# The first input-projection round, two blocks of 128 features at once, becomes two rounds of one block

## The chip, the cores and the metric

The kernel runs on one NeuronCore of a Trainium2 chip. The metric is the device time of one execution in microseconds. It was 1379.97 us as the median of three runs (1379.35 to 1381.22). TensorE (PE) multiplies, VectorE (DVE) and ScalarE (ACT) do the elementwise work, GpSimd (POOL) issues some loads, and SyncE (SP) issues most of them.

## The reference, cut to what matters

One layer of a hybrid trunk is run for two streams of 128 tokens: a prompt (conditioning `c_ctx`) and a sample (conditioning `c`). The part that the change touches is its beginning:

```python
mod = jax.nn.silu(cvec) @ w_ada_l + b_ada_l            # 2048 -> 6 x 2048
sh1, sc1, g1, sh2, sc2, g2 = jnp.split(mod[..., None, :], 6, axis=-1)
h = modulate(rmsnorm(x, norm_w), shift, scale)         # h * (1 + scale) + shift, width 2048
p = h @ w_in_l                                         # 2048 -> 8192, split over the mixers
```

Behind it come a gated linear recurrence, a short convolution and a neighbourhood attention, their output projection, a second modulation and a SwiGLU channel mixer. All is float32.

## The kernel before, in words

All tensors stand with 128 partitions. A product in float32 accuracy is three TensorE products: weights and activations are each split into a rounded part `hi` and a rest `lo`, and hi*hi, hi*lo and lo*hi are summed. For each loaded weight tile `raw`, ACT writes `hi` (L253) and DVE `lo` (L254). The activations of the two streams stand in `hT`, four tiles of four blocks of 128 features; in each, slot 0 is `hi` and slot 1 is `lo`.

The modulation of the first norm is itself a product with weights: `ada_pe` (L318) multiplies one quarter of the 2048 conditioning features (four times 128) with 256 columns of shift and 256 of scale. I call one such call a quarter: eight matmuls 32 rows high and 256 columns wide, one load of 1 MB. Four quarters give shift and scale of 256 features (two blocks). ACT copies the result out (L338), `columns` (L341) turns it so that features stand on partitions, DVE adds the biases (L351 to L353), ACT applies scale and shift to the transposed normalised x (L484), and ACT and DVE split the result into `hT` (L488, L489).

The input projection has 16 chunks of 512 output columns. The first seven (`ORDER[:START]`) are worked in rounds over the features, since the modulation of the later features is not there yet. `ROUNDS` lists (first block, number of blocks): (0,2), (2,2), (4,4), (8,4), (12,4). In a round each of the seven chunks loads the rows of its weights for these blocks (256 KB per block), multiplies them for both streams (six matmuls of 512 columns for each block), and the two sums leave PSUM: in the first round ACT copies them into `part` (L880), in the later ones DVE adds them to it (L882). Between the chunks of a round `first_step` puts the quarters that the next round needs. The other nine chunks, and all behind them, follow without rounds.

Four things limit how far the work runs ahead. `raw` has four buffers, and each load, small or large, takes a whole one; SP issues the loads in order, and each waits for the release of the buffer four loads before it. `hi` and `lo` have three buffers each. PSUM has four sums (`acc`, two chunks), three `aux` tiles and one `ada`. Each engine works through its instructions in the order in which a scheduler put them at build time.

At the very start SP issues, in this order, the two conditioning vectors, the first quarter, x of the prompt, x of the sample (1 MB each) and three quarters; these four quarters take all four `raw` buffers. ACT squares x (L503), DVE makes the reciprocal root (L201 to L207) and normalises (L505), and PE transposes (L471).

Of the kernel before, what the change touches and what calls it, by code (L numbers as in the profile page):

```python
# [10 lines left out]
F32 = mybir.dt.float32  # L11
# [13 lines left out]
NEG = -1.0e30  # L25
RMS1 = -8192.0
START = 7
ROUNDS = [(0, 2), (2, 2), (4, 4), (8, 4), (12, 4)]


LATER_T = [12, 16, 13, 17, 14, 18, 15, 19]
# [61 lines left out]
def trunk(ctx: ExitStack, tc: tile.TileContext, a: dict):  # L93
# [144 lines left out]
    def split(src, apart=False):  # L238

        n = src.shape[1]  # L240
        with tc.high_priority(offset=ahead[0]):
            raw = sb([P, 4, CH], "raw", RAW_BUFS)
            nc.sync.dma_start(raw[:, 0:n], src)
            parts = []
            if apart:
                his, los = u8((P, 4, CH), F32R), u8((P, 4, CH), F32R)
            for j in range(n // 2):
                if apart:
                    hi, lo = his[:, 2 * j:2 * j + 2], los[:, 2 * j:2 * j + 2]
                else:  # L250
                    hi = sb([P, 2, CH], "hi", HL_BUFS, F32R)
                    lo = sb([P, 2, CH], "lo", HL_BUFS, F32R)
                nc.scalar.activation(hi, raw[:, 2 * j:2 * j + 2], AF.Copy)  # L253
                nc.vector.tensor_tensor(lo, raw[:, 2 * j:2 * j + 2], hi.bitcast(F32), op=ALU.subtract)  # L254
                parts.append((hi, lo))
        return parts

# [12 lines left out]
    def split_mm(src, acc, lhs, first, last, k0=0):  # L270

        parts = split(src)
        n = src.shape[1]
        for k in range(0, n, 2):
            products([(s, acc[s]) for s in range(2)], (k, k + 1), lhs, k0, parts, first and k == 0, last and k == n - 2)

    def last_mm(steps, acc, phase):

# [37 lines left out]
    def ada_pe(src, box, part, pieces, first, last):  # L316

        if first:  # L320
            uid[0] += 1
            box["acc"] = psum.tile([P, CH], F32, tag="ada", name=f"ada_{uid[0]}", bufs=1)
        with tc.high_priority(offset=ahead[0]):
            if part in box:
                raw = box[part]
            else:
                raw = sb([P, 4, CH], "raw", RAW_BUFS)
                nc.sync.dma_start(raw, src)
                raw = [raw[:, 0:2], raw[:, 2:4]]
        for k in range(4):  # L330
            for i, (cols, row) in enumerate(pieces):
                nc.tensor.matmul(box["acc"][32 * k:32 * k + 32, 0:cols.stop - cols.start],  # L332
                                 lhsT=cst[:, 4 * part + k, 2 - row:34 - row], rhs=raw[k // 2][:, k % 2, cols],
                                 start=first and i == 0, stop=last and i == len(pieces) - 1)
        if last:
            n = cols.stop - cols.start
            e = st()
            nc.scalar.activation(e[:, 0:n], box["acc"][:, 0:n], AF.Copy)  # L338
            return e

    def columns(e, n):  # L341

        ps = aux((P, n, 4))
        for f in range(n):
            nc.tensor.matmul(ps[:, f, :], lhsT=e[:, f * P:(f + 1) * P], rhs=sel4, start=True, stop=True)
        return ps[:, :, 0:2], ps[:, :, 2:4]

    def first_fm(v, e):
        sh, sc = columns(e, 2)
        blk = slice(2 * v, 2 * v + 2)  # L350
        nc.vector.tensor_tensor(sh_fm[1][:, blk, :], sh, bc_last(bsh[:, 0, blk], 2), op=ALU.add)  # L351
        nc.vector.tensor_tensor(sc_fm[1][:, blk, :], sc, bc_last(bsh[:, 1, blk], 2), op=ALU.add)
        nc.vector.scalar_tensor_tensor(sc_fm[1][:, blk, :], sc_fm[1][:, blk, :], 1.0, bc_last(nmw[:, blk], 2),  # L353
                                       op0=ALU.add, op1=ALU.mult)
# [109 lines left out]

    def norm_fm(xn, diag=None):

        ps = aux((P, 2, 2, P))
        for s in range(2):
            for j in range(2):
# [6 lines left out]
    def modulated(dst, ps, layer, v):  # L476

        h = st((P, 2, 2, P))
        for s in range(2):
            for j in range(2):  # L480
                k = 2 * v + j
# [25 lines left out]

    hT = [None] * 4

    def first_mod(v, part, box):  # L510

        e = ada_pe(a["w_ada1"][v, part], box, part, PAIR, part == 0, part == 3)
        if part == 3:
            spawn(first_done(v, e, norm_fm([x[:, 256 * v:256 * v + 256] for x in xt])))

    def first_done(v, e, ps):
        yield
        first_fm(v, e)
        if v % 2 == 0:
            hT[v // 2] = u8(dt=F32R)  # L520
        modulated(hT[v // 2], ps, 1, v)

    COL = {"hg0": 8, "hg1": 9, "ff0": 4, "ff1": 5, "fb0": 6, "fb1": 7, "q0": 0, "q1": 1, "v0": 2, "v1": 3,
           "cb": 10, "cc": 11, "cx": 12, "nq": 13, "nk": 14, "nv": 15}
# [330 lines left out]
            S["late"] = {"f": lambda: S["K", int(name[2])][:, :, 0, :], "q": lambda: S["qT", int(name[1])][:, 0:2, :],  # L855
                         "n": lambda: S["nq"][:, :, 0, :], "c": lambda: S["cc"][:, :, 0, :]}[name[0]]()

    firsts = [(v, p) for v in range(8) for p in range(4)][1:]

    def first_step(n):  # L860
        for v, p in firsts[:n]:
            first_mod(v, p, box)
# [95 lines left out]
    for q in range(4):  # L958
        for j in range(2):
            ps = norm_fm([x1[q][:, s, 256 * j:256 * j + 256] for s in range(2)], r2)  # L960
            modulated(h2[q], ps, 2, 2 * q + j)

    S["late"] = h2[3].bitcast(F32)[:, :, 1, 0, :]

# [156 lines left out]
```

## Time and profile before

| | |
|---|---|
| median of three runs | 1379.97 us (1379.35 to 1381.22) |
| the profiled execution | 1374.68 us, its span 1372.9 us |
| PE | 1338.6 us busy, 97% of the span |
| DVE, ACT, POOL | 872.9 us (64%), 627.4 us (46%), 132.6 us (10%) |
| mean granted TensorE clock | 0.995 |
| HBM read | 330.43 MB, 243 GB/s over the span |

The profiled execution is 5.3 us shorter than the median of the runs; sums made in the trace are compared with its own 1374.68 us. A busy share is a mean over stages with different limits; what matters below is which engine waits in the first 100 us and for what. The time of one matmul in a row is its latency; the rate is read from the length of a chain and its count.

### The profile page before, as it was taken

The numbers are of one execution on the slowest core, as the hardware profiler recorded it, in microseconds if no ns is written. First come the engines' busy times: TensorE is split into PE (matmuls) and PEld (weight loads), VectorE is DVE, ScalarE is ACT, GpSimd is POOL, SyncE is SP. The second block draws the span as 40 slices with busy tenths as digits, with TensorE's granted clock in tenths as the row PEclk, the third lists the DMA queues.
The fourth block names the chain that finished last, engine by engine and source line by source line (L and its number), as shares of the span: only waits on it lengthen the run. The fifth ranks groups of instructions, "written<-read, shape, count | busy, mean of one in ns | idle before, by whom it ended". The sixth has DMA issues, their size and how long they took to land. (4 is left out here: it accounts for less than half of the span.)

```text
span 1372.9 us, 19781 instructions
## 1 busy us (share of the span) xinstructions
PE 1338.6 (97%) x7936; PEld 1078.0 (79%) x7936; DVE 872.9 (64%) x1102; ACT 627.4 (46%) x839; POOL 132.6 (10%) x201
## 2 busy tenths in 40 slices
PE   5999999999999999999999999999999999999996
PEld 3667777797798897778788888888888888888885
DVE  3355558986977687477944888655555554455564
ACT  4433447655465443446444444444334444444442
POOL 0100001131222221001200222000000000000000
PEclk9999999999999999999999999999999999999998
DMA  8898976875787889865765677555555555555551
GB/s 349 304 357 305 343 296 220 306 289 200 290 303 254 312 313 357 311 262 192 268 227 187 219 271 245 214 184 189 203 201 207 190 192 197 184 184 186 204 193 62
DMA packets 54381, 335.39 MB, mean 244 GB/s; under 512 B 7249, under 2 KB 7313, under 8 KB 19217
## 3 DMA queue, kind: packets, MB, share of 16 engines
q1 hardware_dynamic: 42768, 296.79, 59.0%
q0 software_dynamic: 10944, 36.29, 7.6%
q8 instruction: 62, 1.02, 0.3%
q10 hardware_dynamic: 576, 1.05, 0.2%
q14 instruction: 31, 0.25, 0.0%
HBM read 330.43 MB, written 3.67 MB: 243 GB/s over the span
## 5 line engine op out<-in xcount | busy, mean ns | idle before, releaser
L267 PE MATMUL acc<-hi,u 128*128 128x512 f32 x2944 | 741.2, 393 | 2.0 <-ACT u L488 1.1
L254 DVE TENSOR_TENSOR lo<-raw,hi 128x1024 fp32r<-128x1024 f32 x368 | 448.6, 1223 | 346.5 <-ACT hi L253 339.2
L267 PEld LDWEIGHTS acc<-hi,u 128*128 128x128 f32 x2944 | 548.7, 188 | 138.1 <-issue 10.4
L253 ACT ACTIVATE hi<-raw 128x1024 fp32r<-128x1024 f32 x368 | 388.8, 1060 | 544.2 <-PE acc L267 426.7
L267 PE MATMUL acc<-lo,u 128*128 128x512 f32 x1472 | 397.1, 390 | 1.8 <-DVE lo L254 1.7
L267 PEld LDWEIGHTS acc<-lo,u 128*128 128x128 f32 x1472 | 275.5, 188 | 63.0 <-DVE lo L254 3.7
L415 DVE SCALAR_TENSOR_TENSOR aacc<-araw,cs,aacc 128x512 f32<-128x512 f32 x224 | 159.0, 746 | 42.9 <-DMA araw<-w_ada 38.8
L308 PE MATMUL acc<-u,hi 128*128 128x256 f32 x768 | 142.2, 286 | 0.0
L308 PEld LDWEIGHTS acc<-u,hi 128*128 128x128 f32 x768 | 119.2, 191 | 9.7 <-issue 5.0
L308 PE MATMUL acc<-u,lo 128*128 128x256 f32 x384 | 108.3, 286 | 0.0
L332 PE MATMUL ada<-raw,cst 128*32 128x256 f32 (+1 forms) x784 | 83.7, 484 | 11.3 <-DMA raw<-w_ada 11.3
L298 ACT ACTIVATE hi<-raw 128x1024 fp32r<-128x1024 f32 x48 | 50.9, 1059 | 63.7 <-PE acc L308 34.5
L308 PEld LDWEIGHTS acc<-u,lo 128*128 128x128 f32 x384 | 72.8, 191 | 5.0 <-issue 4.2
L411 POOL COPY araw<-u 128x2 f32<-128x2 f32 x56 | 51.4, 920 | 257.7 <-DVE aacc L415 195.6
L299 DVE TENSOR_TENSOR lo<-raw,hi 128x1024 fp32r<-128x1024 f32 x48 | 58.2, 1218 | 15.3 <-ACT hi L298 12.0
L332 PEld LDWEIGHTS ada<-raw,cst 128*32 128x32 f32 x784 | 23.8, 114 | 38.0 <-issue 27.7
L882 DVE TENSOR_TENSOR u<-u,acc 128x512 f32<-128x512 f32 x56 | 35.9, 682 | 25.0 <-PE acc L267 24.9
L412 POOL DMA_DIRECT2D araw<-w_ada x56 | 30.0, 536 | 15.0 <-POOL araw L411 14.4
L405 POOL COPY aacc<-u 128x2 f32<-128x2 f32 x7 | 3.2, 453 | 266.6 <-DVE u L882 163.6
L484 ACT ACTIVATE st<-aux,sh,sc 128x128 f32<-128x128 f32 x48 | 18.1, 455 | 12.8 <-DVE sc L353 10.6
L267 PE MATMUL acc<-u,u 128*128 128x512 f32 x96 | 22.1, 389 | 0.0
L267 PEld LDWEIGHTS acc<-u,u 128*128 128x128 f32 x96 | 18.0, 188 | 3.7
(218 smaller groups left out, 627.0 us busy)
## 6 DMA issues: line engine op xcount, KB each, us to landing
raw<-w_ada SPq DMA_DIRECT2D x66, 1024.0 KB, 7.1
raw<-w_gate SPq DMA_DIRECT2D x44, 1024.0 KB, 4.8
raw<-w_up SPq DMA_DIRECT2D x44, 1024.0 KB, 4.8
raw<-w_down SPq DMA_DIRECT2D x44, 1024.0 KB, 4.8
raw<-w_in SPq DMA_DIRECT2D x33, 1024.0 KB, 6.8
araw<-w_ada POOLq DMA_DIRECT2D x56, 512.0 KB, 5.9
raw<-w_infm SPq DMA_DIRECT2D x24, 1024.0 KB, 5.6
raw<-w_out SPq DMA_DIRECT2D x16, 1024.0 KB, 7.2
```

What stands on the lines that cost most here:

```text
L253: nc.scalar.activation(hi, raw[:, 2 * j:2 * j + 2], AF.Copy)
L254: nc.vector.tensor_tensor(lo, raw[:, 2 * j:2 * j + 2], hi.bitcast(F32), op=ALU.subtract)
L267: nc.tensor.matmul(acc, lhsT=lhs[:, s, x, k0 + k, :], rhs=w[:, k % 2, :], start=first and k == ks[0] and w is hi and x == 0, stop=last and ...
L298: nc.scalar.activation(hi, raw[:, 4 * j:4 * j + 4], AF.Copy)
L299: nc.vector.tensor_tensor(lo, raw[:, 4 * j:4 * j + 4], hi.bitcast(F32), op=ALU.subtract)
L308: nc.tensor.matmul(one, lhsT=w[:, k % 4, ws], rhs=y, start=first and k == 0 and i == 0, stop=last and k == 7 and i == 2)
L332: nc.tensor.matmul(box["acc"][32 * k:32 * k + 32, 0:cols.stop - cols.start], lhsT=cst[:, 4 * part + k, 2 - row:34 - row], rhs=raw[k // 2][ ...
L411: nc.gpsimd.tensor_copy(raw[:, :, 0:1], S["late"][:, :, 0:1])
L412: nc.gpsimd.dma_start(raw, a["w_ada2"][c - 8, part // 2, :, 2 * (part % 2):2 * (part % 2) + 2, :])
L415: nc.vector.scalar_tensor_tensor(acc[:, s, :], raw[:, k, :], cs[:, 2 * part + k, s:s + 1], acc[:, s, :], op0=ALU.mult, op1=ALU.add)
L484: nc.scalar.activation(h[:, s, j, :], ps[:, s, j, :], AF.Identity, bias=bias, scale=scale)
L882: nc.vector.tensor_tensor(part[name][:, s, :], part[name][:, s, :], acc[s], op=ALU.add)
```

## The change

The list of rounds begins with two rounds of one block. So that the first of them does not need the modulation of both blocks, the shift and scale of blocks 0 and 1 are now made apart: each by four half quarters (128 columns of shift and 128 of scale, a load of 512 KB) from a new array `w_ada0`, in which the columns are laid out accordingly. Loads, splits, transposes and modulation take the number of blocks as an argument. A half quarter's load writes 1 KB pieces (256 columns of each of four rows) into the 2 KB rows of a `raw` buffer. The weights of one block are a load of 256 KB.

```diff
-ROUNDS = [(0, 2), (2, 2), (4, 4), (8, 4), (12, 4)]
+ROUNDS = [(0, 1), (1, 1), (2, 2), (4, 4), (8, 4), (12, 4)]
...
-            for j in range(n // 2):
+            for j in range((n + 1) // 2):
+                m = min(n, 2)
...
-                nc.scalar.activation(hi, raw[:, 2 * j:2 * j + 2], AF.Copy)
-                nc.vector.tensor_tensor(lo, raw[:, 2 * j:2 * j + 2], hi.bitcast(F32), op=ALU.subtract)
+                nc.scalar.activation(hi, raw[:, 2 * j:2 * j + m], AF.Copy)
+                nc.vector.tensor_tensor(lo, raw[:, 2 * j:2 * j + m], hi.bitcast(F32), op=ALU.subtract)
...
-                nc.sync.dma_start(raw, src)
+                nc.sync.dma_start(raw[:, :, 0:src.shape[2]], src)
...
-    def first_fm(v, e):
-        sh, sc = columns(e, 2)
-        blk = slice(2 * v, 2 * v + 2)
+    def first_fm(k0, n, e):
+        sh, sc = columns(e, n)
+        blk = slice(k0, k0 + n)
...
-        ks = slice(2 * (v % 2), 2 * (v % 2) + 2)
+        ks = slice(k0 % 4, k0 % 4 + n)
...
-    PAIR = [(slice(0, 256), 0), (slice(256, 512), 2)]
-    ada_pe(a["w_ada1"][0, 0], box, 0, PAIR, True, False)
+    def first_ada(k0, n, part):
+
+        src = a["w_ada0"][k0, part] if n == 1 else a["w_ada1"][k0 // 2 - 1, part]
+        return ada_pe(src, box, part, [(slice(0, n * P), 0), (slice(n * P, 2 * n * P), 2)], part == 0, part == 3)
+
+    first_ada(0, 1, 0)
...
-    firsts = [(v, p) for v in range(8) for p in range(4)][1:]
+    firsts = [(k0, n, p) for k0, n in [(0, 1), (1, 1)] + [(k, 2) for k in range(2, 16, 2)] for p in range(4)][1:]
...
-    first_step(4 * ROUNDS[0][1] // 2 - 1)
+    first_step(3)
...
-        nxt = 4 * ROUNDS[ri + 1][1] // 2 if ri + 1 < len(ROUNDS) else 0
+        nxt = 4 * max(ROUNDS[ri + 1][1] // 2, 1) if ri + 1 < len(ROUNDS) else 0
```

The scheduler's order on each engine changes in the first part of the program only: on PE within the first 870 of some 6,900 matmuls, on ACT and DVE within the first 180 instructions, and from there on it is the same; on POOL it is the same from the first to the last instruction. SP has eleven loads more.

On ACT, ahead of the first product of the projection, the order before was this (`hi` is the split of a weight tile, `st` from `ada` the copy of the modulation, `st` from `aux` the modulated x, `u_22` the tile `hT`):

```order
L503 ACTIVATE u_12_131,ssq_11_130<-u_5_112 128x2048
L253 ACTIVATE hi_201<-raw_199 128x1024
L338 ACTIVATE st_176<-ada_99 128x256
L253 ACTIVATE hi_224<-raw_222 128x1024
L484 ACTIVATE st_190<-aux_178,sh_95,sc_97 128x128 x4
L488 ACTIVATE u_22_189<-st_190 128x2x256
L253 ACTIVATE hi_270<-raw_268 128x1024
```

In the changed kernel it is this:

```order
L510 ACTIVATE u_12_131,ssq_11_130<-u_5_112 128x2048
L254 ACTIVATE hi_196<-raw_194 128x512
L339 ACTIVATE st_176<-ada_99 128x128
L254 ACTIVATE hi_213<-raw_211 128x512
L486 ACTIVATE st_187<-aux_178,sh_95,sc_97 128x128 x2
L254 ACTIVATE hi_253<-raw_251 128x512
L490 ACTIVATE u_22_186<-st_187 128x2x128
```

Two modulations stand where four stood, every instruction but the square is half as long, and the split of the third chunk's weights has moved ahead of the copy into `hT`.

On PE, between the first round and the second, the order before was this (`acc` are the chunk sums, `ada` a quarter, `aux` from `sel` the columns, `aux` from `ident` transposes):

```order
L267 MATMUL acc_402<-lo_407,u_22_189 128x512
L267 MATMUL acc_403<-lo_407,u_22_189 128x512
L345 MATMUL aux_425<-sel_72,st_395 128x4 x2
L332 MATMUL ada_460<-raw_461,cst 32x256 x8
L471 MATMUL aux_547<-ident,u_4_110 128x128 x2
L471 MATMUL aux_547<-ident,u_5_112 128x128 x2
L332 MATMUL ada_460<-raw_493,cst 32x256 x8
L267 MATMUL acc_438<-hi_442,u_22_189 128x512
```

In the changed kernel, between its first and second round, it is this:

```order
L268 MATMUL acc_359<-hi_363,u_22_186 128x512 x2
L346 MATMUL aux_376<-sel_72,st_354 128x4
L473 MATMUL aux_525<-ident,u_4_110 128x128 x2
L473 MATMUL aux_525<-ident,u_5_112 128x128 x2
L268 MATMUL acc_359<-lo_364,u_22_186 128x512
L268 MATMUL acc_360<-hi_363,u_22_186 128x512 x2
L268 MATMUL acc_360<-lo_364,u_22_186 128x512
L333 MATMUL ada_418<-raw_419,cst 32x256 x8
L268 MATMUL acc_386<-hi_390,u_22_186 128x512
```

The columns and transposes now stand inside the last chunk of the round, and one quarter instead of two stands between the rounds.

## Rows read from the trace of the kernel before

**Rows 1.** The page: the span and the engines' busy time

```profile
span 1372.9 us, 19781 instructions
...
PE 1338.6 (97%) x7936; PEld 1078.0 (79%) x7936; DVE 872.9 (64%) x1102; ACT 627.4 (46%) x839; POOL 132.6 (10%) x201
```

**Rows 2.** Stages: length, busy of PE, PEld, DVE, ACT, POOL, clock, DMA

```profile
0.00:27.03 27.03, 11.37 (x93) 5.04 (x93) 10.41 (x34) 11.47 (x16) 2.88 (x10) 0.95 0.88 341
27.03:40.00 12.97, 12.97 (x61) 9.68 (x58) 4.07 (x4) 6.60 (x10) 3.85 (x10) 0.84 0.90 342
40.00:57.77 17.77, 16.68 (x116) 10.63 (x115) 5.80 (x10) 11.30 (x20) 0.00 (x0) 1.00 0.84 284
57.77:88.65 30.88, 29.45 (x195) 20.28 (x196) 16.16 (x24) 9.04 (x13) 0.00 (x0) 1.00 0.90 328
88.65:100.00 11.35, 10.58 (x70) 7.44 (x69) 6.18 (x10) 4.98 (x8) 0.00 (x0) 1.00 1.00 406
100.00:200.00 100.00, 100.00 (x610) 74.66 (x609) 57.16 (x76) 41.24 (x55) 0.00 (x0) 1.00 0.85 320
```

**Rows 3.** PE in order of time: the start and the second round's start

```profile
7.15 1.96 PE L332 MATMUL ada<-raw,cst 128*32 128x256 f32 x16 [7.15 <-DMA raw<-w_ada]
...
19.30 0.69 PE L471 MATMUL aux<-ident,u 128*128 128x128 f32 x2
19.92 1.61 PE L332 MATMUL ada<-raw,cst 128*32 128x256 f32 x16
...
22.35 0.61 PE L345 MATMUL aux<-sel,st 128*128 128x4 f32 x4 [0.82 <-ACT st L338]
...
25.14 1.96 PE L332 MATMUL ada<-raw,cst 128*32 128x256 f32 x16 [1.68 <-DMA raw<-w_ada]
27.03 4.53 PE L267 MATMUL acc<-hi,u 128*128 128x512 f32 x10
...
55.00 0.66 PE L471 MATMUL aux<-ident,u 128*128 128x128 f32 x4
...
57.77 1.21 PE L267 MATMUL acc<-hi,u 128*128 128x512 f32 x4 [1.09 <-ACT u L488]
60.41 1.09 PE L332 MATMUL ada<-raw,cst 128*32 128x256 f32 x16 [1.43 <-DMA raw<-w_ada]
...
66.19 1.09 PE L332 MATMUL ada<-raw,cst 128*32 128x256 f32 x16
```

**Rows 4.** ACT and DVE in order of time, first 65 us

```profile
9.74 1.91 ACT L503 ACTIVATE u<-u 128x2048 f32<-128x2048 f32 x1 [5.60 <-DMA u<-xp]
...
12.23 1.91 ACT L503 ACTIVATE u<-u 128x2048 f32<-128x2048 f32 x1 [0.49 <-DMA u<-xs]
...
16.79 1.29 DVE L505 TENSOR_SCALAR u<-u,r_g 128x2048 f32<-128x2048 f32 x1
...
22.06 1.22 DVE L254 TENSOR_TENSOR lo<-raw,hi 128x1024 fp32r<-128x1024 f32 x1 [3.98 <-ACT hi L253]
...
23.46 0.16 DVE L353 SCALAR_TENSOR_TENSOR sc<-sc,nmw 128x4 f32<-128x4 f32 x1
23.66 1.50 ACT L484 ACTIVATE st<-aux,sh,sc 128x128 f32<-128x128 f32 x4 [0.36 <-DVE sc L353]
25.19 0.63 ACT L488 ACTIVATE u<-st 128x512 fp32r<-128x512 f32 x1
...
32.78 1.06 ACT L880 ACTIVATE u<-acc 128x512 f32<-128x512 f32 x2
...
63.81 1.28 DVE L882 TENSOR_TENSOR u<-u,acc 128x512 f32<-128x512 f32 x2 [4.75 <-PE acc L267]
```

**Rows 5.** The chain that ended last: 768 products on end

```profile
905.95 174.10 PE acc L267 x768
```

**Rows 6.** Loads: first 130 us, then the last 8 us: count, size, landing

```profile
raw<-w_ada SPq DMA_DIRECT2D x24, 1024.0 KB, 6.4
...
raw<-w_in SPq DMA_DIRECT2D x14, 512.0 KB, 5.7
...
o_ys<-u SPq DMA_DIRECT2D x2, 256.0 KB, 3.1
```

**Rows 7.** Who waited for whom in the first 100 us

```profile
ACT hi L253 <- DMA raw<-w_in: 35.3, 13, 7.4
```

More of the change, by code (lines that the diff above doesn't have):

```diff
@@ L250, in split @@
                 else:
-                    hi = sb([P, 2, CH], "hi", HL_BUFS, F32R)
-                    lo = sb([P, 2, CH], "lo", HL_BUFS, F32R)
-                nc.scalar.activation(hi, raw[:, 2 * j:2 * j + 2], AF.Copy)
-                nc.vector.tensor_tensor(lo, raw[:, 2 * j:2 * j + 2], hi.bitcast(F32), op=ALU.subtract)
+                    hi = sb([P, 2, CH], "hi", HL_BUFS, F32R)[:, 0:m]
+                    lo = sb([P, 2, CH], "lo", HL_BUFS, F32R)[:, 0:m]
+                nc.scalar.activation(hi, raw[:, 2 * j:2 * j + m], AF.Copy)
+                nc.vector.tensor_tensor(lo, raw[:, 2 * j:2 * j + m], hi.bitcast(F32), op=ALU.subtract)
                 parts.append((hi, lo))
@@ L274, in split_mm @@
         for k in range(0, n, 2):
-            products([(s, acc[s]) for s in range(2)], (k, k + 1), lhs, k0, parts, first and k == 0, last and k == n - 2)
+            products([(s, acc[s]) for s in range(2)], range(k, min(k + 2, n)), lhs, k0, parts, first and k == 0, last and k + 2 >= n)
     def last_mm(steps, acc, phase):
@@ L465, in norm_fm @@
     def norm_fm(xn, diag=None):
-        ps = aux((P, 2, 2, P))
+        n = xn[0].shape[1] // P
+        ps = aux((P, 2, n, P))
         for s in range(2):
-            for j in range(2):
+            for j in range(n):
                 if diag is None:
@@ L474, in norm_fm, with modulated @@
         return ps
-    def modulated(dst, ps, layer, v):
-        h = st((P, 2, 2, P))
+    def modulated(dst, ps, layer, k0, n):
+        h = st((P, 2, n, P))
         for s in range(2):
-            for j in range(2):
-                k = 2 * v + j
+            for j in range(n):
+                k = k0 + j
                 scale, bias = sc_fm[layer][:, k, s:s + 1], sh_fm[layer][:, k, s:s + 1]
@@ L508, in trunk, with first_mod, first_done @@
     hT = [None] * 4
-    def first_mod(v, part, box):
-        e = ada_pe(a["w_ada1"][v, part], box, part, PAIR, part == 0, part == 3)
+    def first_mod(k0, n, part):
+        e = first_ada(k0, n, part)
         if part == 3:
-            spawn(first_done(v, e, norm_fm([x[:, 256 * v:256 * v + 256] for x in xt])))
-    def first_done(v, e, ps):
+            spawn(first_done(k0, n, e, norm_fm([x[:, P * k0:P * (k0 + n)] for x in xt])))
+    def first_done(k0, n, e, ps):
         yield
[L518 to L521, printed above, removed]
+        first_fm(k0, n, e)
+        if k0 % 4 == 0:
+            hT[k0 // 4] = u8(dt=F32R)
+        modulated(hT[k0 // 4], ps, 1, k0, n)
     COL = {"hg0": 8, "hg1": 9, "ff0": 4, "ff1": 5, "fb0": 6, "fb1": 7, "q0": 0, "q1": 1, "v0": 2, "v1": 3,
@@ L856, in consume_fm @@
                          "n": lambda: S["nq"][:, :, 0, :], "c": lambda: S["cc"][:, :, 0, :]}[name[0]]()
-    firsts = [(v, p) for v in range(8) for p in range(4)][1:]
+    firsts = [(k0, n, p) for k0, n in [(0, 1), (1, 1)] + [(k, 2) for k in range(2, 16, 2)] for p in range(4)][1:]
     def first_step(n):
-        for v, p in firsts[:n]:
-            first_mod(v, p, box)
+        for one in firsts[:n]:
+            first_mod(*one)
         del firsts[:n]
-    first_step(4 * ROUNDS[0][1] // 2 - 1)
+    first_step(3)
     pump()
@@ L960, in trunk @@
             ps = norm_fm([x1[q][:, s, 256 * j:256 * j + 256] for s in range(2)], r2)
-            modulated(h2[q], ps, 2, 2 * q + j)
+            modulated(h2[q], ps, 2, 4 * q + 2 * j, 2)
     S["late"] = h2[3].bitcast(F32)[:, :, 1, 0, :]
@@ L1092 @@
     first = w_ada[:, :2 * D].reshape(D, 2, 8, 256).transpose(0, 2, 1, 3).reshape(D, 2 * D)
+    first0 = tiles(first)[0]
     rows = np.concatenate([np.arange(1024), np.arange(1536, 2048), np.arange(1024, 1536)])
@@ L1098 @@
         "s0": x["state_hgrn"][0, 0], "cT": np.ascontiguousarray(fm(cvec).transpose(0, 2, 1)),
-        "w_ada1": tiles(first), "w_ada2": tiles(w_ada[:, 2 * D:]),
+        "w_ada0": np.stack([np.concatenate([first0[..., h * P:h * P + P], first0[..., 256 + h * P:256 + h * P + P]], axis=-1)
+                            for h in range(2)]),
+        "w_ada1": tiles(first)[1:], "w_ada2": tiles(w_ada[:, 2 * D:]),
         "b_ada": x["b_ada"], "bsh": fm(x["b_ada"][0, :2 * D].reshape(2, D)), "nmw": fm(x["norm_mix_w"][0]), "w_in": tiles(w_in),
```

## The prediction

> **What bounds the kernel now.** I read the page first: PE is busy 1338.6 of 1372.9 us [rows 1], so the time is PE's work plus 34.3 us in which PE has none. The stages say where [rows 2]: PE is idle for 15.7 us (27.03 less 11.37) before the first product of the projection at 27.03, for 1.1 us up to 57.77 (the start of the round of blocks 2 and 3), 1.4 us up to 88.65 (the start of blocks 4 to 7), 0.8 us up to 100, and not at all in the 100 us that follow. Besides, the granted clock is at its lower level (1.2 GHz) in part of the second stage, whose mean is 0.84. So PE bounds the kernel from 57.77 on, and only the start can give something back. What is won there should come out at the end as it is: behind the first sixth of each engine's instructions the order is the same as before, and a stage in which PE does not wait moves as a whole.
>
> The order of time on PE shows the start [rows 3]: a quarter at 7.15, three more as their loads land, the last at 19.92; columns at 22.35; then a fifth quarter at 25.14, which already belongs to the next blocks, and the first product. ACT and DVE show what stands between [rows 4]: x of the sample at 12.23, normalised at 18.08 (16.79 + 1.29), shift and scale ready at 23.62, four modulations until 25.16, the copy into `hT` until 25.82. That the fifth quarter fills the wait matters: a first product that is earlier by some us does not win these us, as work that now stands ahead of it has to be done later.
>
> **The change, step by step.** I walk PE forward in the new order with durations of these rows, to a point where both kernels have the same work behind them.
>
> Step 1, the first product. The two loads of x stand 2.49 us apart (12.23 less 9.74) [rows 4], so 1 MB takes 2.49 us there. The first load is half as large, so x of the sample is there at 12.23 - 1.25 = 10.98, and its normalised copy, with the same 5.85 us, at 16.83. The other three half quarters (1.5 MB) land 3.7 us behind x, at 14.7, where 19.92 stood. So the load is no longer last, x is. From 16.83: a transpose (half of 0.69) until 17.2 and columns (half of 0.61) until 17.5. DVE has two splits in front (half of 1.22 each) until 18.1, then three small ones (about 0.46) until 18.6. ACT does two modulations (half of 1.50) until 19.4, then the third chunk's split, which the new order puts in front (0.53, half of the 1.06 for two equally long copies), until 19.9, then the half copy (0.32) until 20.2; 0.3 for the hops between engines. First product: 20.5, which is 6.5 us earlier.
>
> The unknown here is a load that writes 1 KB pieces. One bound is no loss: the 256 KB outputs at the end go in small pieces too and landed in 3.1 us, half of what the larger loads in a full queue took [rows 6]. The other is half speed, as if the empty half of each row were moved too: then the four half quarters take 5.0 us more, the last is there at 19.7, and the first product comes near 23.5 (19.7, 0.7 for itself, 0.2 copy, 0.3, 0.5, 0.75, 0.5, 0.3 and hops), 3 us of the gain gone. I take no loss, since the output row is nearest in size, and keep the other for the range.
>
> Step 2, the round of block 0. A product takes 174.10 / 768 = 0.227 us [rows 5]. A quarter costs 1.25 us: from 60.41 to 66.19 are 5.78 us, and in them 20 products (4.53). A half quarter is between 0.55 (half of 1.09) and 1.25; I take 0.7 (1.25 less half of 1.09). PE has 42 products (9.5), three half quarters (2.1), one quarter (1.25), columns (0.3) and four transposes (0.66): 13.8 us. The clock: the first ten products took 4.53 us where they need 2.27 [rows 3], and the quarter ahead 1.96 instead of 1.09; the same low stretch now costs 2.3 + 0.5. That makes 16.6, and the second round starts at 37.1. Beside it, hidden: ACT with 14 copies and seven splits of 0.53 and a half modulation, 12.4 us; SP with its issues; the adds of the sums are not there yet.
>
> Step 3, the round of block 1. 42 products (9.5), three quarters inside (3.75), columns (0.5), transposes (0.66) and one quarter behind (1.25): 15.7 us. DVE is nearly as long: 14 adds of 0.64, seven splits of 0.61 and the small ones, 14.1 us. These adds are new work (9.0 us, as one more round empties its sums); cover is there, because DVE was busy for 9.9 of the 30.7 us from 27.03 to 57.77 [rows 2], but a split that stands behind four adds makes PE wait. I put 1.1 us for that and for a late quarter; its bounds are 0 and the 2.5 us (1.09 + 1.43) that PE loses at the same place before. The round of blocks 2 and 3 then starts at 53.9.
>
> Step 4, the comparison. At 53.9 PE has done 84 products and 9 quarters (8 half ones count 4). Before, at 57.77, it has done 84 and 10. One quarter more makes 55.15 against 57.77: 2.6 us. Right behind it the kernel before waits 1.43 us for the eleventh quarter's load [rows 3]; in the walk this load is there about 2 us ahead of PE, so that stall goes too: 4.0 us. What is late next is PE itself. Against its own time: 1374.68 - 4.0 = 1370.7, the span 1368.9. The runs stand 5.3 us above the profiled one, so I forecast 1379.97 - 4.0 = 1376.0. About 0.2% (2.8 us) is what a measurement of this kernel can tell from no change.
>
> **The rivals.** First, the clock stays at its upper level (2.4 GHz). Before, it was low in the ten products behind a gap of PE of 1.68 us [rows 3]; in the new start the half quarter of the next block cuts that gap into two of about 1 us. Then the low stretch does not cost its 2.3 us: 1373.7. Against it: PE also does less in each of the first 20 us. TensorE: Matmul & The Clock Gate of the Trainium skill, section What's actually happening, says that the throttled state is the default and activity releases it; no row here shows what shorter gaps do.
>
> Second, DMA takes PE's place and the gain shrinks below what can be measured. ACT waited for weights 35.3 us in the first 100 [rows 7], so loads come just in time already. Up to the last load of round 1 there are 13.5 MB (x 2, eight half quarters 4, four quarters 4, 14 loads 3.5), in my walk landed at 48.2, and by the start of blocks 4 to 7 another 12.5 MB. PE wants that at 88.65 - 4.0 - 1.1 (a split) = 83.6, which needs 0.353 MB/us. The stage up to 88.65 moved 328 GB/s and the one behind it 406 [rows 2]. At 406 the data is 4 us early; at 328 it takes 38.1 us, and blocks 4 to 7 start at 87.4: a gain of 1.3, 1378.7. For it speaks the stage's own number; against it that PE hardly waited there, so that the buffers, not the DMA, set the 328. Half-speed 1 KB pieces end near the same time.
>
> Third, slower: the ring of four `raw` buffers limits the two small rounds. A load of 256 KB takes as much of it as one of 1 MB. From 20.5 to 53.9 there are 22 loads, 1.52 us each, so a buffer may take 6.1 us from its issue to the next. If a load lands in 6.4 us as the large ones do, with its two splits (0.53 and 0.61) it takes 7.54, 1.47 too long: 22 x 1.47 / 4 = 8.1 us are lost, 4.1 slower, 1384.1. It decides from 6.8 us on (no gain; slower by 0.2% from 7.3); with the 5.7 us of the 512 KB loads [rows 6] it is just there. For it speaks that half the bytes landed only 0.7 us sooner; against it, that a small load waits behind fewer bytes, and 3.1 us were enough for 256 KB. A rule speaks for this rival: the Trainium skill's DMA: Bandwidth & Descriptors, section Measured (HBM to SBUF), asks for loads of at least 1 MiB for 75% of the peak, and its section Anatomy of one DMA gives each load about 2.0 us besides its bytes. By that, if nothing of the fixed part overlapped, the eleven added loads would cost an estimated 22 us, which would make the kernel some 18 us slower. The trace agrees only in part, since 341 GB/s over a first stage of mixed sizes [rows 2] show that fixed parts overlap while several loads are in flight.
>
> **How the numbers follow.** The forecast gets 0.46; its own range is 1374.5 to 1377.5 (waits of step 3 between its bounds, half quarter between its bounds). The clock gets 0.15, DMA 0.28, the ring 0.11. Faster by over 0.2%: 0.39 of the forecast's 0.46, all of the clock's 0.15, 0.02 of the DMA's, 0.56. Slower: 0.11. The rest, 0.33, within 0.2%. The range 1373.2 to 1380.6 leaves out the ring and the lower half of the clock's case.
>
> **What would show it.** In the changed profile the first product should stand at 20.5 (19.5 to 22), directly behind ACT's copy and not behind a load; the granted clock should return to 2.4 GHz near 25; the second round should start near 37.1, the round of blocks 2 and 3 near 53.9, that of blocks 4 to 7 near 84.6. DMA should be less than half busy around 25 to 32 and full from 50 to 80. Behind 100 us every stage should be as long as before. Wrong would be: a first product near 23.5 (1 KB pieces); PE waiting for ACT's splits in the two small rounds with DMA idle (the ring), or in blocks 2 and 3 with DMA full (the DMA); or a stage behind 100 us that is longer by some us.

## The result, and the profile after

The changed kernel takes 1391.92 us (median of four runs, 1389.4 to 1393.61); the kernel before took 1379.66 us beside it. The ratio is 1.0087, 95% interval 1.0064 to 1.0111: slower by 12.3 us, where 1376.0 was forecast. The two profiled executions stand further apart (1393.53 and 1374.68 us), because that of before lies 5 us under its median; sizes below are taken from medians where there are any.

The page, and the stages cut as in [rows 2] (length; busy time of PE, PEld, DVE, ACT, POOL; clock; DMA share; GB/s):

```profile
span 1391.8 us, 19970 instructions
...
PE 1348.9 (97%) x8000; PEld 1082.1 (78%) x8000; DVE 882.3 (63%) x1127; ACT 628.9 (45%) x848; POOL 128.4 (9%) x201
```

```profile
0.00:27.03 27.03, 11.30 (x109) 7.07 (x110) 9.67 (x35) 10.14 (x15) 2.88 (x10) 1.00 0.78 263
27.03:40.00 12.97, 11.00 (x75) 8.02 (x73) 4.81 (x11) 10.35 (x21) 3.31 (x10) 1.00 0.80 229
40.00:57.77 17.77, 15.54 (x103) 10.07 (x104) 11.06 (x18) 4.76 (x10) 0.00 (x0) 0.90 0.88 295
57.77:88.65 30.88, 28.69 (x206) 18.93 (x206) 17.90 (x28) 10.85 (x17) 0.00 (x0) 1.00 0.99 360
88.65:100.00 11.35, 9.82 (x61) 6.89 (x62) 5.55 (x9) 6.66 (x11) 0.00 (x0) 0.85 0.93 382
100.00:200.00 100.00, 100.00 (x588) 70.97 (x588) 52.45 (x67) 34.78 (x46) 0.00 (x0) 1.00 0.76 300
```

Against [rows 2], DMA moves less in the first 40 us, not more: 263 and 229 GB/s where it moved 341 and 342. Only in the third stage is it slightly more, 295 where it moved 284. PE is idle for 4.2 us from 27.03 to 57.77 instead of 1.1. And in the 100 us behind, where PE never waits in either kernel, it passes 588 instructions instead of 610. The same stretch of time need not hold the same work in both, but counted by products (below) the loss is there too: something has become longer without a wait. These are two separate losses.

PE in order of time, to hold against [rows 3]:

```profile
22.87 2.08 PE L268 MATMUL acc<-hi,u 128*128 128x512 f32 x4 [1.92 <-ACT u L490]
...
40.87 1.48 PE L333 MATMUL ada<-raw,cst 128*32 128x256 f32 x16 [2.84 <-DMA raw<-w_ada]
42.29 2.82 PE L268 MATMUL acc<-hi,u 128*128 128x512 f32 x6
...
61.64 2.18 PE L268 MATMUL acc<-hi,u 128*128 128x512 f32 x8
```

The first product is early, at 22.87. The second round starts only at 42.29, behind 2.84 us of waiting for a quarter's load, and the round of blocks 2 and 3 at 61.64, 3.9 us later than before. The chain that ended last holds the 768 products of [rows 5] with the same 174.10 us, 19.54 us later:

```profile
925.49 174.10 PE acc L268 x768
```

Who waited for whom in the first 100 us, on PE and on SP's queue (in total, times, longest), first in the kernel before, then in the changed one:

```profile
PE ada L332 <- DMA raw<-w_ada: 10.3, 3, 7.2
...
SPq L243 <- PE ada L332: 16.5, 10, 3.0
```

```profile
PE ada L333 <- DMA raw<-w_ada: 18.4, 7, 6.5
...
SPq L243 <- PE ada L333: 27.4, 14, 3.7
```

SP stands 27.4 us with a load of projection weights (L243) that may not be issued until PE has used up the quarter that holds the buffer, four loads earlier; before it was 16.5 us.

### The profile page after: what moved, and what is told of

Same layout as the page of the kernel before. It is cut to its first block, busy times and chain, and to the rows that moved or that the text cites. A ratio compares the mean times of both kernels' runs of the same rounds, so it can differ in the third digit from the quotient of the medians.

```text
span 1391.8 us, 19970 instructions
## 1 busy us (share of the span) xinstructions
PE 1348.9 (97%) x8000; PEld 1082.1 (78%) x8000; DVE 882.3 (63%) x1127; ACT 628.9 (45%) x848; POOL 128.4 (9%) x201
## 4 chain that ended last, share of the span: by engine, by line
PE 85%; DMA 7%; issue 3%; DVE 2%; POOL 1%; ACT 1%; SPq 0%; POOLq 0%; DVEq 0%; ACTq 0%
PE acc L268 69%; PE acc L309 8%; PE ada L333 5%; DMA araw<-w_ada 3%; DMA raw<-w_ada 2%; PE aux L457 1%; DMA raw<-w_in 1%; POOL araw L412 1%; DMA aacc<-b_ada 1%; PE aux L637 0%; DVE aacc L416 0%; PE aux L380 0%; DVE lo L255 0%; PE aux L346 0%; PE aux L691 0%
## 5 line engine op out<-in xcount | busy, mean ns | idle before, releaser
L255 DVE TENSOR_TENSOR lo<-raw,hi 128x1024 fp32r<-128x1024 f32 (+1 forms) x375 | 449.5, 1203 | 326.3 <-ACT hi L254 312.7
L254 ACT ACTIVATE hi<-raw 128x1024 fp32r<-128x1024 f32 (+1 forms) x375 | 389.9, 1044 | 557.4 <-PE acc L268 428.6
L333 PE MATMUL ada<-raw,cst 128*32 128x256 f32 (+2 forms) x848 | 88.1, 457 | 20.2 <-DMA raw<-w_ada 20.1
L299 ACT ACTIVATE hi<-raw 128x1024 fp32r<-128x1024 f32 x48 | 50.6, 1059 | 63.6 <-PE acc L309 37.2
L889 DVE TENSOR_TENSOR u<-u,acc 128x512 f32<-128x512 f32 x70 | 45.1, 683 | 46.3 <-PE acc L268 46.3
L300 DVE TENSOR_TENSOR lo<-raw,hi 128x1024 fp32r<-128x1024 f32 x48 | 58.4, 1222 | 14.8 <-ACT hi L299 11.8
L333 PEld LDWEIGHTS ada<-raw,cst 128*32 128x32 f32 x848 | 27.3, 114 | 50.6 <-issue 25.2
```

Source lines behind the costliest of these rows:

```text
L254: nc.scalar.activation(hi, raw[:, 2 * j:2 * j + m], AF.Copy)
L255: nc.vector.tensor_tensor(lo, raw[:, 2 * j:2 * j + m], hi.bitcast(F32), op=ALU.subtract)
L299: nc.scalar.activation(hi, raw[:, 4 * j:4 * j + 4], AF.Copy)
L300: nc.vector.tensor_tensor(lo, raw[:, 4 * j:4 * j + 4], hi.bitcast(F32), op=ALU.subtract)
L889: nc.vector.tensor_tensor(part[name][:, s, :], part[name][:, s, :], acc[s], op=ALU.add)
```

## Experiments

All were timed beside the kernel before, which took 1378.8 to 1381.1 us in these sets. A ratio below is to the kernel before of the same set; medians of different sets are less comparable. In the first four expectations "pieces" are the 1 KB pieces that a half quarter's load writes; in the later ones they are the groups into which PE's order cuts a quarter.

**Each half of the change alone.** Rounds whole, modulation of blocks 0 and 1 in half quarters:

```diff
-ROUNDS = [(0, 1), (1, 1), (2, 2), (4, 4), (8, 4), (12, 4)]
+ROUNDS = [(0, 2), (2, 2), (4, 4), (8, 4), (12, 4)]
-    first_step(3)
+    first_step(7)
```

> The first round takes both blocks again, as in the kernel before; only the modulations of blocks 0 and 1 stay apart (eight half quarters in 1 KB pieces instead of four quarters). Ring theory (the four raw buffers count loads, so the two rounds of small weight loads leave the DMA idle and PE waits): nearly all of the loss of 12.3 us is gone, 1379 to 1383 us. Piece theory (the half quarters and their 1 KB pieces cost the time): most of the loss stays, 1388 to 1392. Extra-round theory (one more round with its boundary and its adds costs PE directly): 1379 to 1382.

Measured: 1388.53 us, ratio 1.0057 (1.0041 to 1.0073). Rounds of one block with whole quarters:

```diff
-        src = a["w_ada0"][k0, part] if n == 1 else a["w_ada1"][k0 // 2 - 1, part]
+        src = a["w_ada1"][k0 // 2, part]
-    first_ada(0, 1, 0)
+    first_ada(0, 2, 0)
-        nxt = 4 * max(ROUNDS[ri + 1][1] // 2, 1) if ri + 1 < len(ROUNDS) else 0
+        nxt = (2, 2, 8, 8, 8, 0)[ri]
```

> The two rounds of one block stay, but blocks 0 and 1 are modulated together by four whole quarters as in the kernel before, two later quarters in each of the two rounds. Ring theory: the first product comes near 26 to 27 us, the loads of 256 KB still hold a raw buffer each, 1386 to 1392 us. Piece theory: 1379 to 1382. Extra-round theory: 1385 to 1392, with PE waiting at the boundary between the two rounds and not inside them; under the ring theory it waits for loads inside them and in the round of blocks 2 and 3.

Measured: 1389.45 us, 1.0077 (1.0056 to 1.0098), inside the numbers of the ring and of the extra round. Each half costs most of the whole, so neither is the cause by itself; what they share comes first into question. The ring's number for the first was missed: its eight half quarters take whole buffers too, and its order has the same new groups on PE (below).

**The 1 KB pieces.** The half quarter lands in one run of 4 KB per partition:

```diff
-                nc.sync.dma_start(raw[:, :, 0:src.shape[2]], src)
+                raw = raw.rearrange("p k n -> p (k n)")[:, 0:4 * src.shape[2]].rearrange("p (k n) -> p k n", k=4)
+                nc.sync.dma_start(raw, src)
```

> The changed kernel, but a half quarter's load writes the buffer in one piece of 4 KB per partition instead of four of 1 KB. Piece theory: the first product comes 2 to 3 us earlier (near 20.5) and most of the loss goes, 1380 to 1386 us. Ring theory: at most 1 to 2 us, 1389 to 1392, with the idle stretches of the DMA between 20 and 37 us as before. Extra-round theory: 1391 to 1392.

Measured: 1391.25 us, 1.0078 (1.0060 to 1.0095). The first product comes 0.9 us earlier than in the changed kernel (21.98), not 2 to 3, and in this kernel the pieces cost no time that can be told at the end. They do cost DMA rate while DMA is the limit, which it is from 10 to 15 us (before, then the changed kernel):

```profile
10.00:15.00 5.00, 0.00 (x0) 0.00 (x0) 2.91 (x11) 3.75 (x4) 0.00 (x0) 1.00 1.01 421
```

```profile
10.00:15.00 5.00, 1.63 (x21) 0.98 (x25) 3.44 (x14) 3.11 (x4) 0.00 (x0) 1.00 1.08 361
```

At a share of 1.08 the 1 KB pieces move 361 GB/s, where whole quarters move 421 at 1.01 and the runs of 4 KB in this experiment move 373 at 0.94.

**The ring.** The one-block loads take buffers of two other tags, with two buffers each, so that the four `raw` buffers hold the quarters:

```diff
+            if n == 1:
+                small[0] += 1
+                raw = sb([P, 2, CH], ("ld", "araw")[small[0] % 2], 2)
+            else:
                 raw = sb([P, 4, CH], "raw", RAW_BUFS)
```

> The changed kernel, but the weight loads of the two rounds of one block go to four other buffers that have no work yet (those of the later input loads), so that the raw buffers hold modulation loads alone there. Ring theory: the DMA stays busy from 20 to 40 us, the first product comes near 21 us, the round of blocks 4 to 7 near 88, and most of the loss is gone: 1377 to 1383 us. Piece theory and extra-round theory: as the changed kernel, 1389 to 1393.

Measured: 1382.1 us, 1.0014 (1.0000 to 1.0027): 9.8 us of the 12.3 are back. The extra round and its adds are all still there, so they are not what cost the time. The DMA page of 20 to 40 us (share in tenths and GB/s in 40 slices, then the sum), of the changed kernel and of this one:

```profile
DMA  3689997436988256421038999999899479679989
...
DMA packets 2863, 4.61 MB, mean 230 GB/s; under 512 B 273, under 2 KB 1826, under 8 KB 2735
```

```profile
DMA  9999999999999899899998999989999999999999
...
DMA packets 3222, 7.53 MB, mean 377 GB/s; under 512 B 323, under 2 KB 1811, under 8 KB 2732
```

The same loads wait for a buffer in the first kernel, where DMA falls under a tenth near 29.5 us, and fill the DMA in the second. The 2.9 MB that are missing after 40 us take 7.7 us at 377 GB/s. With the loads in time, PE comes near the prediction's walk: the first product stands at 20.86 (20.5 in the walk), the second round at 38.7 (37.1), the round of blocks 2 and 3 at 53.5 (53.9) and that of blocks 4 to 7 at 86.6 (84.65), where before had 88.65 and the changed kernel 96.80.

The clock column shows the lower level (1.2 GHz) nowhere in the first 100 us of this run, and in the changed kernel from 41.4 to 44.9 and from 92.6 to 96.1, behind gaps of PE of 2.84 and 1.00 us. At full speed these two stretches would take about half (an estimate: 3.4 us less); this is a part of what the ring costs there. But the first products are slow in this run too, 0.46 us each for the first six:

```profile
20.86 2.93 PE L273 MATMUL acc<-hi,u 128*128 128x512 f32 x6 [0.84 <-ACT u L495]
23.59 0.74 PE L273 MATMUL acc<-lo,u 128*128 128x512 f32 x2
```

**The quarters on PE.** 2 us over before are left with the spare tags, and the place is seen by counting products (line of the products, busy time and count from 0 to a moment; before, then the changed kernel, then this one):

```profile
0.00:88.00 88.00, 44.03 (x168) 32.00 (x168) 0.96 0.88 326
0.00:236.50 236.50, 166.68 (x672) 124.48 (x672) 0.99 0.84 315
```

```profile
0.00:97.00 97.00, 47.86 (x169) 33.65 (x170) 0.96 0.89 308
0.00:252.00 252.00, 172.07 (x672) 125.33 (x672) 0.99 0.80 295
```

```profile
0.00:86.50 86.50, 44.79 (x168) 31.16 (x168) 1.00 0.93 338
0.00:241.50 241.50, 169.09 (x672) 123.13 (x672) 1.00 0.82 308
```

From product 168 to 672 before takes 148.5 us, both others 155, and so do the two halves of the change (155.5 and 155). PE's order of the quarters there differs: the same 141 matmuls stand in 19 groups between products before, in 24 in all of these, and they hold PE for 27.9 us instead of 22.3. PE in order of time, before and after:

```profile
103.12 1.09 PE L332 MATMUL ada<-raw,cst 128*32 128x256 f32 x16
104.14 1.21 PE L267 MATMUL acc<-hi,u 128*128 128x512 f32 x4
```

```profile
108.15 1.05 PE L333 MATMUL ada<-raw,cst 128*32 128x256 f32 x6
109.14 1.21 PE L268 MATMUL acc<-lo,u 128*128 128x512 f32 x4
110.28 1.07 PE L333 MATMUL ada<-raw,cst 128*32 128x256 f32 x10
111.28 2.11 PE L268 MATMUL acc<-hi,u 128*128 128x512 f32 x8
...
116.03 0.62 PE L333 MATMUL ada<-raw,cst 128*32 128x256 f32 x2
116.58 1.20 PE L268 MATMUL acc<-lo,u 128*128 128x512 f32 x4
...
153.80 1.06 PE L333 MATMUL ada<-raw,cst 128*32 128x256 f32 x8
154.79 0.73 PE L268 MATMUL acc<-hi,u 128*128 128x512 f32 x2
```

(A matmul of a quarter leaves two records, so x16 is the quarter's eight.) From its start to the next start a whole quarter takes 1.02 us; cut into 6 and 10 records it takes 0.99 and 1.00, and one half of it, 8 records, 0.99. A single matmul takes 0.55. To see whether the cuts make the 155, the quarters' matmuls were given a higher priority, with which the scheduler cuts fewer (21 groups), in three kernels:

```diff
-        for k in range(4):
-            for i, (cols, row) in enumerate(pieces):
+        with tc.high_priority(offset=400):
+            for k in range(4):
+                for i, (cols, row) in enumerate(pieces):
```

On the changed kernel, its ring as it was:

> Edit: the changed kernel, ring of four raw buffers kept, with only the higher priority for the quarters' matmuls: from the 168th to the 504th product 16 groups instead of 19; the first 168 products keep 6, 4 and 7 groups as in the changed kernel.
> Piece theory: 3 to 4 us less than the changed kernel, 1387 to 1389; from product 168 to 672 about 151 to 152 us; the waits for w_ada before product 168 (about 18 us) stay.
> Rival, ring theory alone (all of the loss is the wait for loads before product 168): no gain, 1391 to 1392.

Measured: 1386.61 us, 1.0047 (1.0031 to 1.0063); 148.0 us from product 168 to 672, with 22.8 us of PE for the quarters. On the kernel with the spare tags:

> Edit: the kernel with the two spare tags for single-block loads, and the 141 matmuls of the quarters issued at a higher priority, so that PE's order cuts fewer quarters in two: from the 168th to the 504th product the quarters stand in 16 groups instead of 19 (before the change 14), behind it in 5 as before.
> Piece theory (a quarter that the order cuts into more groups costs about 1 to 1.3 us per extra group): from product 168 to product 672 it takes about 151 to 152 us instead of 155, and the time falls from 1382.1 to 1378 to 1380.
> Rival, extra-load theory (the 6.5 us between these products do not come from the cuts, but from what the deeper load pattern leaves behind): still 155 us there, time 1381 to 1383.

Measured: 1377.56 us, 0.9990 (0.9971 to 1.0009); 147.5 us. Both stages are shorter than the 151 to 152 us expected, and no longer than before's although 21 groups stand where 19 stood: the 21 are 16 whole quarters and 5 whole groups of a later modulation on the same line (four matmuls of 512 columns each). So it is the cuts that cost, not the number of groups. The two cures add up about: 9.8 for the ring, 5.3 for the cuts, 14.4 for both. On the kernel before:

> Edit: the kernel before, same loads, same buffers, quarters' matmuls at the higher priority: on the whole of PE's order the quarters stand in 66 groups instead of 72.
> Piece theory (0.95 us of TensorE time per group, from 121 groups and 130.3 us against 72 groups and 83.7 us): TensorE time of the quarters 77 to 79 us, time 1373 to 1376.
> Ring theory alone: groups do not matter, 1379 to 1381.

Measured: 1378.55 us, 0.9990 (0.9968 to 1.0012). The piece theory's time was missed: the quarters' TensorE time fell from 83.7 to 76.4 us, but the time hardly. PE asks for the quarters earlier there and waits 17.7 us for their loads over the run, instead of 11.3, and for DVE in two later places (3.8 and 3.3). And with offset 30, which cuts more:

> Edit: the kernel before, same loads and same buffers, only the quarters' matmuls at a slightly higher priority, which here cuts them into more groups: behind product 168 4, 4, 13 and 7 instead of 4, 3, 7 and 5 (28 against 19); before product 168 21 against 18.
> Piece theory (1 to 1.3 us per group): from product 168 to 672 157 to 160 us instead of 148.5, time 1389 to 1394.
> Rival (a cut costs next to nothing, what differs is elsewhere): 148 to 150 us there, time 1379 to 1382.

Measured: 1433.08 us, 1.0380 (1.0358 to 1.0401), far over both numbers. In this stage it lost only 5 us (153.5), as many of its pieces are single matmuls, which are cheap; the rest comes from the later part of the program, which the edit cuts too. All quarters of the run, before and here (busy us, mean ns):

```profile
L332 PE MATMUL ada<-raw,cst 128*32 128x256 f32 (+1 forms) x784 | 83.7, 484 | 11.3 <-DMA raw<-w_ada 11.3
```

```profile
L333 PE MATMUL ada<-raw,cst 128*32 128x256 f32 (+1 forms) x784 | 130.3, 486 | 16.1 <-DMA raw<-w_ada 16.1
```

The same 784 records in 121 groups instead of 72 hold PE 46.6 us longer, 0.95 us per group, and the run is 53 us longer.

**Why a cut costs that much.** Either each change between the two kinds of matmul has a fixed price, or the four matmuls of different column groups (the 32 output partitions `32 * k`) run beside each other, and a piece is as long as a column group that has both of its matmuls in it. The loops are exchanged, so that a piece of four has one of each:

```diff
-        for k in range(4):
-            for i, (cols, row) in enumerate(pieces):
+        for i, (cols, row) in enumerate(pieces):
+            for k in range(4):
```

> Edit: the changed kernel with the two loops of a quarter's matmuls exchanged: first the four column groups' matmuls for shift, then the four for scale, where each column group had its shift and its scale on end. The same matmuls, loads and buffers; the order of the rest moves slightly (22 groups of quarters behind product 168 instead of 24).
> Column theory (the four 32-column groups of a quarter run beside each other, each with two matmuls on end, so a piece of 2 to 8 matmuls lasts 1.0 us and one matmul 0.55): a piece of up to four matmuls of different column groups now lasts 0.5 to 0.65 us, a whole quarter still 1.0 to 1.1; from product 168 to 672 150 to 152 us instead of 155, time 1386 to 1389.
> Rival, fixed price (each change between 128-row products and 32-row matmuls costs about 1 us by itself): pieces of 2 to 4 matmuls last 1.0 us as before, 153 us for two groups fewer, time 1389 to 1391.

Measured: 1385.23 us, 1.0034 (1.0013 to 1.0055), and 148.5 us from product 168 to 672. PE in order of time:

```profile
104.34 0.64 PE L333 MATMUL ada<-raw,cst 128*32 128x256 f32 x8
104.91 1.20 PE L268 MATMUL acc<-lo,u 128*128 128x512 f32 x4
...
127.57 1.07 PE L333 MATMUL ada<-raw,cst 128*32 128x256 f32 x16
128.57 1.21 PE L268 MATMUL acc<-lo,u 128*128 128x512 f32 x4
```

Half a quarter, the same 8 records, now takes 0.57 us instead of 0.99, and a whole one 1.00, so two halves cost 0.14 over the whole, where 6 and 10 records cost 0.97. A fixed price near 1 us is out; the gain is slightly above what the column theory expected. The Trainium skill says the same in TensorEngine Tiling (Array Packing), Key Properties: different tiles of the array can work in parallel. By that, four matmuls on four column groups last as long as one, and the trace agrees: 0.57 for four, 0.55 for one.

**What the early start is worth.** The same tags for the two-block loads, once on the kernel before (`if n == 2`) and once on the changed one (`if n <= 2`), without and with the priority:

> Edit: the kernel before, with only the loads of the two-block rounds sent to the two other tags (so that the ring of four holds quarters alone there). PE's groups of quarters behind product 168 are those of before (4, 3, 7, 5); between product 84 and 168 there are 7 instead of 9.
> Ring theory: PE's waits for w_ada before product 168 fall from about 4 us to under 1 (the first wait at 8 us stays), product 168 starts at 84 to 86 instead of 88; piece theory: two groups fewer are worth 2 more, and from 168 to 672 it takes 148 to 149 us as before. Together 1375 to 1378 against 1380.
> Rival (the loads were paced by the memory and not by buffers): within 1 us of before, 1379 to 1381.

> Edit: the changed kernel with the loads of both one-block rounds and of the two-block round on the two other tags, priorities as they were: 72 groups of quarters against 70 of the kernel before with the same tags.
> If the one-block start is worth its earlier products once ring and groups are out of the way: 1372 to 1376 against 1374.8 (3 us earlier at product 168, 2 us back for two groups).
> Rival (the extra half quarters, 64 more matmul records of 0.13 to 0.17 us beside their groups, and the interleaving eat it): 1376 to 1380.

> Edit: the kernel before with the two-block rounds' loads on the two other tags and the higher priority for the quarters' matmuls: 65 groups against 70 with the tags alone.
> Piece theory: about 5 us under the tags alone (1374.8), 1369 to 1371.
> Rival (waits for loads come back where the quarters are asked for earlier): 1373 to 1376.

> Edit: as the one before, with the higher priority for the quarters' matmuls: 66 groups against 65 of the kernel before with both edits.
> If the one-block start is worth its earlier products: 1367 to 1370, 1 to 3 us under the kernel before with both edits.
> Rival (it is worth nothing): level with it or up to 3 us over it, 1370 to 1373.

Measured: before with the tags 1374.78, ratio 0.9964 (0.9950 to 0.9978); changed 1376.34, 0.9978 (0.9962 to 0.9994). With the priority too: 1376.51, 0.9976 (0.9961 to 0.9992), missed by 5 us as above, and 1376.01, 0.9973 (0.9953 to 0.9994), missed as well. No gain for the early start shows in either pair. The tags alone make the kernel before faster by 5.5 us too, so its ring also held loads back, and not all of the 9.8 us above is a cost of the change. The tags and the exchanged loops together, first on the kernel before:

> Edit: the same exchange on the kernel before with the two-block rounds' loads on the two other tags; 19 groups behind product 168 as there.
> Column theory: few quarters are cut in unequal pieces there, so little to win: 147 to 148.5 us from product 168 to 672, time 1372 to 1375 (1374.8 without the exchange).
> Rival, fixed price: no difference, 1374 to 1376. If whole quarters become longer (the exchange breaks the overlap): over 1.2 us each and 1378 or more.

Measured: 1371.87 us, 0.9935 (0.9915 to 0.9954), the best version. Then both on one chip:

> Edit: the changed kernel with the loads of both one-block rounds and the two-block round on the two other tags, and the quarters' two loops exchanged: both causes of the loss are out of the way, and 19 groups of quarters stand behind product 168, as in the kernel before with the same two edits (1371.87).
> If the one-block start were worth what was predicted once nothing else is in its way: 1367 to 1369, 3 to 4 us less than that.
> Rival (the loads set the pace of the first 85 us in both, so the early products only wait later): level, 1371 to 1375; product 168 within 1.5 us of the other's 84.0, DMA share of the first 85 us over 0.95.

> Edit: the kernel before with the two-block rounds' loads on the two other tags and the quarters' loops exchanged, as already run, beside the one above on the same chip.
> Both theories: 1370 to 1374; if it lies 3 us or more over the one above, the early start is worth something by itself, and if within 1.5 us, nothing that can be measured.

Measured: 1375.4 us, 0.9970 (0.9953 to 0.9987), for the one-block start, and 1371.73, 0.9946 (0.9929 to 0.9963), for the two-block start. With both causes out of the way the early start does not win the 4 us; its median is 3.7 us behind, more than the rival's "level", though the intervals of the two ratios overlap. The stages of the two (0 to 20, 20 to 40, 40 to 57, 57 to 70 us), one-block start first:

```profile
0.00:20.00 20.00, 7.05 (x86) 4.15 (x86) 8.79 (x34) 9.77 (x15) 2.89 (x10) 1.00 0.89 293
20.00:40.00 20.00, 19.75 (x135) 13.44 (x136) 5.98 (x13) 11.92 (x25) 3.77 (x10) 1.00 1.02 378
40.00:57.00 17.00, 15.46 (x125) 8.98 (x123) 12.94 (x24) 5.34 (x11) 0.00 (x0) 1.00 1.00 391
57.00:70.00 13.00, 10.79 (x67) 7.81 (x68) 7.46 (x12) 6.45 (x10) 0.00 (x0) 0.87 1.01 415
```

```profile
0.00:20.00 20.00, 6.64 (x60) 2.79 (x64) 7.04 (x28) 7.01 (x8) 2.88 (x10) 1.00 0.87 344
20.00:40.00 20.00, 15.21 (x92) 10.55 (x81) 5.72 (x8) 9.38 (x16) 3.28 (x10) 0.83 1.02 399
40.00:57.00 17.00, 17.00 (x120) 11.40 (x116) 6.65 (x10) 9.60 (x16) 0.00 (x0) 1.00 0.97 379
57.00:70.00 13.00, 12.74 (x86) 9.11 (x79) 7.86 (x10) 6.41 (x10) 0.00 (x0) 1.00 0.89 330
```

DMA is full from 20 to 57 us in both, so what PE starts earlier it waits for later: from 40 to 70 us PE is idle for 3.8 us in the new start and for 0.3 in the other, and the clock falls to its lower level again (mean 0.87 from 57 to 70). Besides, the new start moves 293 GB/s in the first 20 us against 344, 1.0 MB less at about the same share; at 378 GB/s that is 2.7 us. The 1 KB pieces are still in it, and the same start with runs of 4 KB was not run with these two edits; so how much of the 3.7 us is theirs, and whether the early start would then win anything, stays open. The lead of 6.3 us at the first product is 4.4 at the 42nd, none at the 84th, and 3 us of lag at the 168th.

## Why the prediction was wrong, by its steps

Two terms of the sum failed. The wait for late loads was put at 1.1 us, within bounds of 0 and 2.5, where a ring of four buffers that is counted in loads made the round of blocks 2 and 3 start 7.7 us behind the walk. And the work behind the start was put at no change, where quarters cut by the new order cost 6.5 us between products 168 and 672.

- **Step 1, first product 20.5.** Measured 22.87, under the bound for slow pieces, but for another reason: ACT's split of the third chunk waited until 21.88 for its load. With the spare tags and the same 1 KB pieces it is 20.86. The step's other terms come to within 0.4 us together; the ring reached into it, and this accounts for 2.4 of the 7.7 us.
- **Step 2, second round at 37.1.** Measured 42.29. The half quarter was well priced (0.59 at full clock against 0.7). What was missing is the wait of 2.84 us behind a full ring. In the first products the clock cost about what was put: four products from 22.87 take 2.0 us to the next start, over twice the 0.227 each of [rows 5], although the clock column reads 1.00 there.
- **Step 3, 53.9, with 1.1 us for "a late quarter".** This is the step that failed. Measured 61.64, another 2.6 us on the walk. The walk moved PE forward and let every load but a late quarter be there. The third rival had the right mechanism: from 22.87 to 61.64 the 22 loads took 1.76 us each, so a buffer took 7.05 us on average from issue to issue, over the 6.8 from which that rival said it decides. It was given 0.11 because small loads were expected to land in 3.1 to 5.7 us. They did land in 5.2; but the quarters among the 22 loads land later, as the loads of 20 to 60 us show (count, size, median landing). The rival also ended its sum at blocks 2 and 3, where the changed kernel is 3.9 us behind before; at the start of blocks 4 to 7 it is 8.15 (96.80 against 88.65). So its 1384.1 was too low as well. The 18 us that stand beside it, from a fixed price for each of the eleven added loads, did not come either: with the spare tags the same loads are there, and 2 us are left.

```profile
raw<-w_ada SPq DMA_DIRECT2D x6, 1024.0 KB, 7.3
raw<-w_in SPq DMA_DIRECT2D x10, 256.0 KB, 5.2
```

- **Step 4, "what is won there should come out at the end as it is".** The order changed within PE's first 870 matmuls, the "first sixth", and this was taken for the start alone. These matmuls reach to about 205 us. The stage behind 100 us that "is longer by some us" was named as what would show it wrong, and it came: 6.5 us from product 168 to 672, from cuts whose cost the walk did not count. A quarter had one price, 1.25 us, however the order cuts it; but its matmuls run beside each other, so each unequal piece costs about as much as a whole quarter.
- **The gain of 4.0 itself.** It rested on buffers, not DMA, setting the 328 GB/s of [rows 2]. That was right: with more buffers the kernel before gains 5.5 us. But the change keeps these buffers. With more of them DMA runs full at 377 to 399 GB/s, and the two starts do not differ in the forecast's direction; not even the 1.3 us of the DMA rival are there. That rival's sum also takes a load of 1024 KB for 1 MB: with 1.049 its 12.5 MB are 13.1, and at 328 GB/s they take 40.0 us, which leaves no gain.
- **The clock rival** did not come true. With the spare tags no lower level is recorded, but the first six products there take 0.46 us each, so the column hides a slow stretch, as it does in the changed kernel.

What stays open: in the profiled pair 4 us more come between product 672 and the 768 products, with the same order in both. Single runs of one kernel spread by up to 14 us (1379.36 to 1393.4 with the exchanged loops), and no run here was made to settle these 4.

## What to carry to other kernels

Count a ring of buffers in loads, not in bytes: halving the loads halves the bytes in flight, so before work is cut finer, multiply the loads by issue-to-release time and divide by the buffers. Walk the loads forward as strictly as the engine. And when a scheduler moves work, compare where it cuts groups of the smaller matmuls as far as the order differs at all; a group whose matmuls run beside each other is best written so that a cut in the middle leaves every column group once in each piece.

## What was not expected of the hardware

- Four float32 matmuls of 32 rows and 256 columns on four column groups last 0.57 us together, two to eight with two on one column group 0.98 to 1.02, one 0.55.
- Loads of 256 KB among those of 1 MB kept 377 GB/s from 20 to 40 us with eight buffers in use, and 230 with four. Most of the 7.53 MB came in the large loads; loads of 512 KB and 1 MB alone moved 399 GB/s in the same stretch. The Trainium skill (DMA: Bandwidth & Descriptors, Measured) asks for at least 1 MiB per load for 75% of the peak; the trace does not bear that out for small loads among large ones, where the number in flight made the difference.
- Half quarters in 1 KB pieces moved 361 GB/s at a DMA share of 1.08, whole quarters 421 at 1.01.
- The granted clock reads 1.00 from 22.87 to 27.8 us in the changed kernel while products take 0.4 to 0.5 us, about the rate that [rows 3] show at 1.2 GHz. The kernel before has it too: the quarter at 7.15 takes 1.96 us, not 1.09, at a reading of 1.00. In both it is ahead of the first lower level that the column shows (24.5 us before, 41.4 in the changed kernel).
